# A mixer block's first stage: sums of z products written between the multiply and the low rows, tables last, latents in pairs of rows, and group sums by TensorE

## The chip, the core and the metric

The kernel runs on one core of a Trainium2 chip. A core has five engines that run side by side, each taking its own instructions in order: TensorE (PE in the profile; PEld is its weight load), VectorE (DVE), ScalarE (ACT), GpSimd (POOL) and SyncE (SP). SP and POOL issue DMAs, which 16 DMA engines carry out. An engine that needs another's result waits on a semaphore. The metric is the device time of one execution in microseconds, and the number given is the median over several executions.

## The reference

The block takes 512 latent tokens of width 2048 and 256 context tokens. A conditioning vector gives shift, scale and gate for every channel, and each token is normalized and modulated:

```
shift, scale, gate = split(silu(c) @ w_ada + b_ada, 3)
h = rmsnorm(x, norm_g) * (1 + scale) + shift
p = h @ w_in                       # 2048 -> 9216 columns
y_a = (attention(q, k, v of p and of the context) * silu(z_a)) @ w_proj_a
y_b = (fourier_mix(u_b) * silu(z_b)) @ w_proj_b
out = rmsnorm(x + gate * ((sig(g_a) * y_a + sig(g_b) * y_b) @ w_out), final_g)
```

Two groups of columns of `p` matter here: `u_b` (512 columns), which the Fourier mixing takes, and `z_b` (512 columns), its SiLU gate. The first stage computes both and, on the way, the modulated tokens `h` that all later stages read.

## The kernel before

The latents come in transposed, `xT`, so that channels lie on the 128 partitions. The 2048 channels are 16 blocks of 128, called rows here: row `kb` is a tile of 128 channels by 512 tokens. All products are made at close to float32 accuracy from three float32r matmuls: each operand is split into a high part (ScalarE, L176) and a low remainder (DVE, L177), and `mm3` (L327 to L329) adds high x high, high x low and low x high into one PSUM accumulator.

**Start.** `load_x` asks SP for the latents in the pieces that the list `XCH` gives: six loads of 2, 2, 4, 4, 2 and 2 rows. `token_norms` squares each row (ScalarE L522 and L526, for the second row of four of the pairs DVE L524), adds the two squares of a pair (DVE L527) and sums over partitions with a matmul by ones (L528). The roots are spread over the partitions (L539) and copied to `rx` (L709).

**Rows.** For each row `kb`, `modulate` runs 16 float32 matmuls of the conditioning vector with that row's part of `w_ada` (L551). The vector is padded to 32 columns and the matmuls fall on four groups of 32 partitions, so that the result, 256 columns wide, has four groups of partial sums, of which two partitions each (latents and context) hold numbers. ScalarE copies it out (`ado`, L567). `columns` has TensorE transpose its two halves (`turned`, L571), DVE adds the four groups (L579) and forms `gain` (L580) and `shift` (L582) for the row's 128 channels. The high part of the modulated row then comes from ScalarE, the low part from DVE: for rows 0 to 5 by `by_root` (L594), `row_hi` (L598) and `row_lo` (a multiply, L602, and the low part, L603), for rows 6 to 15 by `make_h` (a multiply, L609, ScalarE's L610, the low part, L611). For rows from 8 on `form_row` adds row differences that a later stage uses (L619 to L621).

**Products of the first stage.** `start_work` is a generator that multiplies the rows, as they become ready, with eight tiles of 128 columns: four of u, four of z. The u tiles have four PSUM accumulators of their own that stay open over all 16 rows (`pb`). The z tiles take turns on two accumulators (`pc`, `bank3`), for one row or two rows (for rows 12 to 15 four) at a time; each partial product is added to its running sum in SBUF (`part`) by `keep`: for row 0 ScalarE's copy (L631), later DVE's add (L633). That add frees the accumulator. `some(n)` runs the generator for `n` steps, of which a step is one tile. `hold` and `release` put one z sum off to a later place in the written order.

**The order.** In this stage the order of TensorE, ScalarE and DVE is the order in which the program is written (L701 and on). From row 6 on, the rows come in rounds of two, and a round has twelve steps: three, then the split of the next weight tile (`split_next`), the first row's modulation, two steps, its columns and its making, three steps, a split, the second row's modulation, one step (the first of four z tiles), its columns, its making and its differences, and three steps, the other z tiles. In the last round the splits of the Fourier tables (`split_table`, and the one of `dftc`) stand ahead of these three. SP issues the loads of `w_ada` and of the weight tiles in written order too, each when its buffer is free.

Of the kernel before, what the change touches and what calls it, by code (L numbers as in the profile page):

```python
# [10 lines left out]
F32 = mybir.dt.float32  # L11
F32R = mybir.dt.float32r
ACT = mybir.ActivationFunctionType
ALU = mybir.AluOpType
AX = mybir.AxisListType
# [3 lines left out]
P = 128  # L19
# [3 lines left out]
KK = D // P  # L23
# [78 lines left out]

XCH = [(0, 2), (2, 2), (4, 4), (8, 4), (12, 2), (14, 2)]


def start_pieces():
# [11 lines left out]
def block_kernel(ctx, tc, xT, ctx_rows, ctx_toks, x, c_row, w_ss, w_gate, vecs, qkg, rope, dft_c, dft_s,  # L120
                 w_start, w_g, w_pab, w_o, final_g, out):
    nc = tc.nc
# [29 lines left out]
    def uid(s):  # L152
        cnt[0] += 1
        return f"{s}{cnt[0]}"
# [278 lines left out]
    q = NGATE  # L433
# [61 lines left out]

    c2 = pap.tile([P, KK, 32], F32, name="c2")
    nc.vector.memset(c2, 0.0)
    rt = pap.tile([P, 1], F32, name="rt")
    ce = pap.tile([P, 2 * KK], F32, name="ce")
    with tc.issue_after(nc.scalar.activation(ce, cvt, ACT.Exp, scale=-1.0).ins):  # L500
# [10 lines left out]
    def token_norms():  # L511

        t = hm_tile([P, 2, T], F32, name=uid("nm"))
        pick, r = t[:, 0, :].rearrange("p (t c) -> p t c", t=4), t[:, 1, :P]
        nc.gpsimd.memset(pick, 0.0)
        for t in range(4):
            nc.gpsimd.memset(pick[32 * t : 32 * t + 1, t, :], 1.0)
        acc = bank2()
        for q in range(0, KK, 2):
            two = hm_tile([P, 2, T], F32, name=uid("sq"))  # L520
            a, b = two[:, 0, :], two[:, 1, :]
            nc.scalar.activation(a, xt[:, q, :], ACT.Square)  # L522
            if q in (4, 8, 10, 14):
                nc.vector.tensor_tensor(b, xt[:, q + 1, :], xt[:, q + 1, :], op=ALU.mult)  # L524
            else:
                nc.scalar.activation(b, xt[:, q + 1, :], ACT.Square)  # L526
            nc.vector.tensor_tensor(a, a, b, op=ALU.add)  # L527
            nc.tensor.matmul(acc, ones, a, start=q == 0, stop=q == KK - 2)  # L528

        for t in range(4):  # L530
            k = slice(32 * t, 32 * t + 32)
            nc.scalar.activation(r[k], acc[k, t * P : t * P + P], ACT.Sqrt, bias=eps_t[k, 0:1], scale=1.0 / D)
        nc.vector.reciprocal(r, r)
        return pick, r
# [22 lines left out]
    def modulate(kb, meanwhile=lambda: None):  # L557
        two[kb] = bank2()
        for h in range(2):
            matvec(kb, h)  # L560
        meanwhile()
        return taken(kb)
# [5 lines left out]

    def turned(sp, o):
        for i in range(2):  # L570
            nc.tensor.transpose(sp[:, P * i : P * i + P], o[:, P * i : P * i + P], ident)  # L571

    def columns(kb):
        sp, o = two.pop(kb)[:, 256:], o_of.pop(kb)
        turned(sp, o)
        if kb == 0:
            warm(3, o)
        r = pap.tile([P, 2, 2], F32, tag="ada_r", bufs=2, name=uid("adr"))
        nc.vector.tensor_reduce(r, sp.rearrange("p (h g r) -> p h r g", h=2, g=4)[:, :, 0:2, :], axis=AX.X, op=ALU.add)  # L579
        nc.vector.tensor_scalar(gain[:, kb, :], r[:, 1, :], bsc1[:, kb : kb + 1], ng[:, kb : kb + 1],  # L580
                                op0=ALU.add, op1=ALU.mult)
        last = nc.vector.tensor_scalar(shift[:, kb, :], r[:, 0, :], bada[:, kb : kb + 1], None, op0=ALU.add)  # L582
        return last

    rx0, y_of = [], {}
# [10 lines left out]
    def row_hi(kb):  # L596
        rows_of(kb)
        nc.scalar.activation(hhi[kb], y_of[kb], ACT.Identity, bias=shift[:, kb, 0:1], scale=gain[:, kb, 0:1])  # L598

    def row_lo(kb):  # L600
        v = xt[:, kb, :]
        nc.vector.tensor_scalar(v, y_of.pop(kb), gain[:, kb, 0:1], None, op0=ALU.mult)  # L602
        nc.vector.scalar_tensor_tensor(hlo[kb], v, shift[:, kb, 0:1], hhi[kb].bitcast(F32),  # L603
                                       op0=ALU.add, op1=ALU.subtract)

    def make_h(kb):
        rows_of(kb)
        v = xt[:, kb, :]
        nc.vector.scalar_tensor_tensor(v, v, gain[:, kb, 0:1], rx if kb else rx0[0], op0=ALU.mult, op1=ALU.mult)  # L609
        act = nc.scalar.activation(hhi[kb], v, ACT.Identity, bias=shift[:, kb, 0:1])  # L610
        return nc.vector.scalar_tensor_tensor(hlo[kb], v, shift[:, kb, 0:1], hhi[kb].bitcast(F32),  # L611
                                              op0=ALU.add, op1=ALU.subtract), act

    def form_row(j):

        a, b = xt[:, j, :], xt[:, j + 8, :]
        h, i = divmod(j, 4)
        d = pap.tile([P, 1], F32, tag="d", bufs=2, name=uid("d"))
        nc.vector.tensor_tensor(d, shift[:, j, 0:1], shift[:, j + 8, 0:1], op=ALU.subtract)  # L619
        nc.vector.tensor_tensor(whole["S3", h][:, i, :], a[:, :256], a[:, 256:], op=ALU.subtract)  # L620
        nc.vector.scalar_tensor_tensor(whole["Z5", h][:, i, :], a[:, 256:], d, b[:, 256:], op0=ALU.add, op1=ALU.subtract)  # L621
# [53 lines left out]
    def some(n):  # L675
        for _ in range(n):
            next(work)
# [10 lines left out]
    def split_next():  # L688
        e = next(e for e in ahead if e.out is None and e.kind != "raw")
        split_piece(e)  # L690
        e.raws = []
# [4 lines left out]
    def release():  # L696
        k = held.pop()
        keep(*k)

    E = mybir.EngineType  # L700
    with tc.manual_schedule(engines={E.PE}):  # L701
        norms = token_norms()
        two[0] = bank2()
        matvec(0, 0)
        rx0.append(spread(*norms))
        matvec(0, 1)
        with tc.manual_schedule(engines={E.Activation, E.DVE}):
            split_next()
            nc.scalar.copy(rx, rx0[0])  # L709
            by_root(0)  # L710
            taken(0)
            wada[2] = wada_load(2)
            load_start()
            columns(0)
            row_hi(0)
            row_lo(0)
            split_next()
            by_root(1)
            some(4)
            modulate(1, split_next)  # L720
            wada[3] = wada_load(3)
            load_start()
            some(2)
            columns(1)
            row_hi(1)
            row_lo(1)
            some(2)
            for kb in range(1, 4):
                k = kb + 1
                some(2)  # L730
                by_root(k)
                if kb > 1:
                    split_next()
                modulate(k)
                if kb < 3:
                    wada[k + 2] = wada_load(k + 2)
                    load_start()
                if kb == 1:
                    split_next()
                hold()  # L740
                some(2)
                columns(k)
                row_hi(k)
                release()
                row_lo(k)
                if kb == 3:
                    some(2)
                    by_root(5)
                    modulate(5)
                    for k in (6, 7):  # L750
                        wada[k] = wada_load(k)
                        load_start()
                    hold()
                    some(2)
                    columns(5)
                    row_hi(5)
                    release()
                    row_lo(5)
                else:
                    some(4)  # L760
            for kb in range(4, KK - 4, 2):
                some(3)
                split_next()
                for i in range(2):
                    k = kb + 2 + i
                    if i:
                        some(3)
                        split_next()
                    modulate(k)
                    if k + 2 < KK:  # L770
                        wada[k + 2] = wada_load(k + 2)
                        for _ in range(2 if k + 2 == KK - 3 else 1):
                            load_start()
                    some(2 - i)
                    columns(k)
                    make_h(k)
                    if k >= 8:
                        form_row(k - 8)
                if kb == KK - 6:
                    split_table(0)  # L780
                    split_from(get(("dftc", 0)), fch[:, 0, :], fch[:, 1, :])
                    load_start()
                some(3)
        for i in range(2):
            k = KK - 2 + i
            some(2)
            modulate(k)
            some(2 - i)
            columns(k)
            ins = make_h(k)  # L790
            with behind(ins):
                split_next()
                form_row(k - 8)
            if not i:
                load_start()
        some(1)
        some(8)
# [1162 lines left out]
```

## Time and profile before

| | us |
|---|---|
| median of 3 runs | 1317.34 (1315.83 to 1318.03) |
| profiled execution | 1314.17 |
| its span, first to last instruction | 1312.4 |
| TensorE busy | 1279.8 |
| DVE busy | 997.4 |
| ScalarE busy | 684.9 |

A row of the profile's timeline gives the start, the duration, the engine, the line, the operation, the tile written and the tiles read, the form, and how many instructions were merged into it; in brackets stands how long the engine had been idle and what ended that. A row of the waits gives the total, the number of times and the longest. A matmul's listed duration runs past the start of the next one, as matmuls are pipelined: back to back, those of 512 columns start 0.23 us apart. Tiles are named without numbers: `pd` holds a row's modulation, `pb` and `pc` are the accumulators above, `wa` is `w_ada`, `wr` a raw weight tile, `whi` and `wlo` its parts, and `s` a row's parts.

### The profile page before, as it was taken

How to read it: one execution, taken by the hardware profiler on the slowest of the kernel's cores; microseconds unless marked ns; L12 is line 12 of the kernel's file. 1: busy time of each engine (PE TensorE's matmuls, PEld its weight loads, DVE VectorE, ACT ScalarE, POOL GpSimd, SP SyncE). 2: the span in 40 equal slices, each digit the busy share in tenths (PEclk: the TensorE clock that was granted, in tenths of full speed). 3: DMA queues.
4: the chain of work that ended last, by engine and by line, in shares of the span. 5: the costliest groups of instructions: out<-in, count | busy, mean ns of one | idle time of the engine just before them, and what ended most of it. 6: DMA issues, size and time to landing. Idle time of an engine off the chain costs nothing.

```text
span 1312.4 us, 17551 instructions
## 1 busy us (share of the span) xinstructions
PE 1279.8 (98%) x6522; PEld 1047.6 (80%) x6522; DVE 997.4 (76%) x1303; ACT 684.9 (52%) x1079; POOL 167.8 (13%) x220
## 2 busy tenths in 40 slices
PE   6998999999999999999999999999999999999997
PEld 3665798888888888888888888888888888888885
DVE  5656699979788697667777756687888867887676
ACT  5222555555555555444345454666667645565544
POOL 0000011020112101011011020011110212221210
PEclk9999999999999999999999999999999999999999
DMA  9988566899798888976869897567872899998985
GB/s 385 372 334 328 190 183 174 256 209 295 203 264 266 253 314 254 324 207 166 260 207 265 294 232 252 196 200 234 264 231 91 222 246 239 253 216 229 218 207 173
DMA packets 103622, 318.54 MB, mean 243 GB/s; under 512 B 9808, under 2 KB 32976, under 8 KB 99184
## 3 DMA queue, kind: packets, MB, share of 16 engines
q1 hardware_dynamic: 54480, 197.86, 41.4%
q0 software_dynamic: 26736, 97.14, 34.3%
q10 hardware_dynamic: 22320, 22.42, 5.0%
q8 instruction: 51, 0.84, 0.2%
q14 instruction: 35, 0.29, 0.1%
HBM read 283.30 MB, written 34.09 MB: 242 GB/s over the span
## 4 chain that ended last, share of the span: by engine, by line
PE 91%; DVE 4%; ACT 2%; issue 1%; DMA 1%; SPq 0%; ACTq 0%; DVEq 0%
PE banks L327 10%; PE banks L328 10%; PE banks L329 10%; PE x L329 9%; PE x L328 9%; PE x L327 9%; PE y L329 7%; PE y L327 7%; PE y L328 7%; PE banks L1448 2%; PE pd L551 2%; PE pb L327 2%; PE pb L329 1%; PE pb L328 1%; PE pc L327 1%
## 5 line engine op out<-in xcount | busy, mean ns | idle before, releaser
L176 ACT ACTIVATE whi<-R 128x1024 fp32r<-128x1024 f32 x138 | 145.7, 1058 | 142.2 <-PE banks L329 53.5
L177 DVE TENSOR_TENSOR wlo<-R,whi 128x1024 fp32r<-128x1024 f32 x138 | 167.8, 1221 | 57.0 <-ACT whi L176 56.7
L177 DVE TENSOR_TENSOR wlo<-wr,whi 128x1024 fp32r<-128x1024 f32 (+1 forms) x122 | 147.3, 1212 | 63.6 <-ACT whi L176 63.0
L176 ACT ACTIVATE whi<-wr 128x1024 fp32r<-128x1024 f32 (+1 forms) x122 | 127.5, 1050 | 114.3 <-PE y L329 37.9
L327 PE MATMUL banks<-whi,s 128*128 128x512 f32 x396 | 157.0, 397 | 2.4 <-DVE ev L1015 1.5
L329 PE MATMUL banks<-whi,s 128*128 128x512 f32 x396 | 155.1, 392 | 0.0
L328 PE MATMUL banks<-wlo,s 128*128 128x512 f32 x396 | 155.1, 392 | 0.0
L327 PE MATMUL x<-whi,s 128*128 128x512 f32 x356 | 138.8, 390 | 0.0
L328 PE MATMUL x<-wlo,s 128*128 128x512 f32 x356 | 138.5, 389 | 0.0
L329 PE MATMUL x<-whi,s 128*128 128x512 f32 x356 | 138.5, 389 | 0.0
L329 PE MATMUL y<-whi,s 128*128 128x512 f32 x308 | 119.8, 389 | 0.5 <-DVE s L177 0.5
L327 PE MATMUL y<-whi,s 128*128 128x512 f32 x308 | 120.0, 389 | 0.2 <-DVE cxe L1168 0.2
L328 PE MATMUL y<-wlo,s 128*128 128x512 f32 x308 | 119.8, 389 | 0.0
L280 POOL DMA_DIRECT2D R<-in_w_g x64 | 56.0, 874 | 418.7 <-DVE wlo L177 261.1
L176 ACT ACTIVATE s<-wr 128x512 fp32r<-128x512 f32 (+2 forms) x95 | 61.1, 675 | 66.2 <-DMA wr<-cf_d 16.1
L177 DVE TENSOR_TENSOR s<-wr,s 128x512 fp32r<-128x512 f32 (+2 forms) x95 | 67.9, 747 | 28.8 <-ACT s L176 28.0
L327 PEld LDWEIGHTS banks<-whi,s 128*128 128x128 f32 x396 | 74.4, 188 | 17.9 <-ACT whi L176 1.9
L329 PEld LDWEIGHTS banks<-whi,s 128*128 128x128 f32 x396 | 74.4, 188 | 15.4
L328 PEld LDWEIGHTS banks<-wlo,s 128*128 128x128 f32 x396 | 74.5, 188 | 14.0 <-DVE wlo L177 0.2
L328 PEld LDWEIGHTS x<-wlo,s 128*128 128x128 f32 x356 | 66.8, 188 | 13.9 <-DVE wlo L177 0.2
L329 PEld LDWEIGHTS x<-whi,s 128*128 128x128 f32 x356 | 66.8, 188 | 13.9
L327 PEld LDWEIGHTS x<-whi,s 128*128 128x128 f32 x356 | 66.8, 188 | 13.8
(310 smaller groups left out, 2823.1 us busy)
## 6 DMA issues: line engine op xcount, KB each, us to landing
wr<-in_w_g SPq DMA_DIRECT2D x128, 512.0 KB, 5.3
wa<-in_w_ss SPq DMA_DIRECT2D x32, 1024.0 KB, 8.0
R<-in_w_g POOLq DMA_DIRECT2D x64, 512.0 KB, 7.0
R<-in_w_g SPq DMA_DIRECT2D x32, 512.0 KB, 5.7
wr<-in_w_gate SPq DMA_DIRECT2D x32, 512.0 KB, 4.9
wr<-in_w_o SPq DMA_DIRECT2D x24, 512.0 KB, 7.7
R<-in_w_o POOLq DMA_DIRECT2D x24, 512.0 KB, 9.2
wr<-in_w_pab SPq DMA_DIRECT2D x20, 512.0 KB, 5.8
```

The lines of the kernel that those rows point to most:

```text
L176: first = nc.scalar.activation(hi, src, ACT.Copy)
L177: return first, nc.vector.tensor_tensor(lo, src, hi.bitcast(F32), op=ALU.subtract)
L280: nc.gpsimd.dma_start(chain[e.pc], e.nxt, accum_op=ALU.add)
L327: nc.tensor.matmul(o, ah, bh, start=start, stop=False, skip_group_check=cont)
L328: nc.tensor.matmul(o, ah, bl, start=False, stop=False, skip_group_check=cont)
L329: nc.tensor.matmul(o, al, bh, start=False, stop=stop, skip_group_check=cont)
L551: nc.tensor.matmul(acc[32 * j : 32 * j + 32], c2[:, n, :], w[:, k, :], start=n < 4, stop=n >= KK - 4)
L1448: nc.tensor.transpose(tp[:, k * P : (k + 1) * P], p[:, k * P : (k + 1) * P], ident)
```

## The change

Five edits, all in the first stage:

- `XCH`: the latents come in nine loads, seven of two rows and two of one row. DVE squares the second row of two pairs instead of four, ScalarE the others.
- `turned` and `columns`: a new tile `four` (128 by 2, made once from the identity) has a one wherever a partition's place in its group of 32 is the column's number. Two float32 matmuls with `four` as the moving operand replace the two transposes; they add the four groups on the way, DVE's L579 is gone, and `gain` and `shift` read PSUM.
- `row_lo` is cut in two: the multiply is now `scaled`, and in the rounds of rows 2 and 3 two of the four steps that followed the row stand between it and the low part.
- `make_h` takes a function that it calls between ScalarE's part and the low part. For the second row of each round from row 6 on, one of the three last steps stands there, one behind the low part, one behind the row differences, and the tables come after that.
- In the loop over rows 2 to 4 the weight split is always made inside `modulate`, ahead of ScalarE's copy; for row 2 it stood behind it and behind the issue of the next loads.

```diff
-XCH = [(0, 2), (2, 2), (4, 4), (8, 4), (12, 2), (14, 2)]
+XCH = [(2 * i, 2) for i in range(KK // 2 - 1)] + [(KK - 2, 1), (KK - 1, 1)]
...
+    four = pap.tile([P, 2], F32, name="four")
+    nc.vector.tensor_reduce(four, ident.rearrange("p (g r) -> p r g", g=4)[:, 0:2, :], axis=AX.X, op=ALU.add)
...
-            if q in (4, 8, 10, 14):
+            if q in (6, 10):
...
     def turned(sp, o):
         for i in range(2):
-            nc.tensor.transpose(sp[:, P * i : P * i + P], o[:, P * i : P * i + P], ident)
+            nc.tensor.matmul(sp[:, 2 * i : 2 * i + 2], o[:, P * i : P * i + P], four, start=True, stop=True)
...
-        r = pap.tile([P, 2, 2], F32, tag="ada_r", bufs=2, name=uid("adr"))
-        nc.vector.tensor_reduce(r, sp.rearrange("p (h g r) -> p h r g", h=2, g=4)[:, :, 0:2, :], axis=AX.X, op=ALU.add)
-        nc.vector.tensor_scalar(gain[:, kb, :], r[:, 1, :], bsc1[:, kb : kb + 1], ng[:, kb : kb + 1],
+        nc.vector.tensor_scalar(gain[:, kb, :], sp[:, 2:4], bsc1[:, kb : kb + 1], ng[:, kb : kb + 1],
                                 op0=ALU.add, op1=ALU.mult)
-        last = nc.vector.tensor_scalar(shift[:, kb, :], r[:, 0, :], bada[:, kb : kb + 1], None, op0=ALU.add)
+        last = nc.vector.tensor_scalar(shift[:, kb, :], sp[:, 0:2], bada[:, kb : kb + 1], None, op0=ALU.add)
...
-    def make_h(kb):
+    def make_h(kb, meanwhile=lambda: None):
         rows_of(kb)
         v = xt[:, kb, :]
         nc.vector.scalar_tensor_tensor(v, v, gain[:, kb, 0:1], rx if kb else rx0[0], op0=ALU.mult, op1=ALU.mult)
         act = nc.scalar.activation(hhi[kb], v, ACT.Identity, bias=shift[:, kb, 0:1])
+        meanwhile()
...
                 by_root(k)
-                if kb > 1:
-                    split_next()
-                modulate(k)
+                modulate(k, split_next)
                 if kb < 3:
                     wada[k + 2] = wada_load(k + 2)
                     load_start()
-                if kb == 1:
-                    split_next()
                 hold()
                 some(2)
                 columns(k)
                 row_hi(k)
                 release()
+                scaled(k)
+                if kb < 3:
+                    some(2)
                 row_lo(k)
...
                 else:
-                    some(4)
+                    some(2)
...
                     some(2 - i)
                     columns(k)
-                    make_h(k)
+                    make_h(k, lambda: some(i))
+                    some(i)
                     if k >= 8:
                         form_row(k - 8)
+                some(1)
                 if kb == KK - 6:
                     split_table(0)
                     split_from(get(("dftc", 0)), fch[:, 0, :], fch[:, 1, :])
                     load_start()
-                some(3)
```

More of the change, by code (lines that the diff above doesn't have):

```diff
@@ L598, in row_hi, with scaled @@
         nc.scalar.activation(hhi[kb], y_of[kb], ACT.Identity, bias=shift[:, kb, 0:1], scale=gain[:, kb, 0:1])
+    def scaled(kb):
+        nc.vector.tensor_scalar(xt[:, kb, :], y_of.pop(kb), gain[:, kb, 0:1], None, op0=ALU.mult)
     def row_lo(kb):
         v = xt[:, kb, :]
-        nc.vector.tensor_scalar(v, y_of.pop(kb), gain[:, kb, 0:1], None, op0=ALU.mult)
         nc.vector.scalar_tensor_tensor(hlo[kb], v, shift[:, kb, 0:1], hhi[kb].bitcast(F32),
                                        op0=ALU.add, op1=ALU.subtract)
-    def make_h(kb):
+    def make_h(kb, meanwhile=lambda: None):
         rows_of(kb)
@@ L715, in block_kernel @@
             row_hi(0)
+            scaled(0)
             row_lo(0)
@@ L725, in block_kernel @@
             row_hi(1)
+            scaled(1)
             row_lo(1)
@@ L757, in block_kernel @@
                     release()
+                    scaled(5)
                     row_lo(5)
                 else:
-                    some(4)
+                    some(2)
             for kb in range(4, KK - 4, 2):
```

## The prediction

> **What bounds the kernel now.** I read the page's first part, then busy time by stretch, then TensorE's waits, then the timeline at the longest of them.
>
> ```profile
> span 1312.4 us, 17551 instructions
> PE 1279.8 (98%) x6522; PEld 1047.6 (80%) x6522; DVE 997.4 (76%) x1303; ACT 684.9 (52%) x1079; POOL 167.8 (13%) x220
> ```
>
> TensorE (PE) is the bound: what shortens its busy or idle time shortens the span. The written order that changes covers the first 150 us.
>
> ```profile
> 24.30:73.86 49.56, 48.88 (x376) 32.62 (x376) 31.73 (x60) 16.77 (x26) 0.00 (x0) 1.00 0.97 389
> 73.86:150.22 76.36, 67.95 (x472) 46.99 (x471) 43.80 (x91) 20.26 (x31) 0.00 (x0) 0.96 0.67 259
> ```
>
> Columns: stretch, length, busy us of PE, weight loads, DVE, ACT, POOL, granted clock, DMA share, GB/s. The first stretch keeps PE full and DMA nearly full (0.97). The second leaves PE idle 8.4 of 76.4 us, at a clock below 1, with DMA at 0.67: there is room, and neither DVE (43.8) nor ACT (20.3) is full.
>
> ```profile
> PE pc L327 <- DVE part L633: 8.4, 4, 3.4
> PE y L329 <- DVE s L177: 0.5, 1, 0.5
> ```
>
> The first row (total, times, longest) is all of that idle time: four times PE waits for a z sum (L633), which empties one of the two pc accumulators. The second is PE's only wait between 165 and 300 us. So what the first stage saves reaches the later work.
>
> One of the four, at row 9:
>
> ```profile
> 89.46 0.75 DVE L609 SCALAR_TENSOR_TENSOR xt<-xt,gain,rx 128x512 f32<-128x512 f32 x1
> 89.50 0.39 PE L329 MATMUL pc<-s,wlo 128*128 128x512 f32 x1
> ...
> 90.89 0.39 PE L329 MATMUL pc<-s,wlo 128*128 128x512 f32 x1
> 91.00 0.75 DVE L611 SCALAR_TENSOR_TENSOR s<-xt,shift,s 128x512 fp32r<-128x512 f32 x1 [0.79 <-ACT s L610]
> ...
> 92.47 1.28 DVE L633 TENSOR_TENSOR part<-pc,part 128x512 f32<-128x512 f32 x2
> 93.21 0.50 PE L327 MATMUL pc<-s,whi 128*128 128x512 f32 x1 [1.93 <-DVE part L633]
> ```
>
> The second z product ends at 89.50 + 0.39 = 89.89, the third is issued to 90.89, and the fourth needs the second's accumulator. Its sum stands on DVE behind multiply (L609), a 0.79 us wait for ScalarE, low row (L611) and the row differences (L619 to L621). PE starts again 0.74 us after the pair of sums begins.
>
> **The change, part by part.** *Sums between multiply and low rows (L609, L611).* The multiply ends at 89.46 + 0.75 = 90.21, after the second product. Its sum takes half of 1.28, some 0.65 us, and fits the 0.79 us in which DVE waits for ScalarE: it ends at about 90.9, the low row stays near 91.0, and the fourth product can follow the third at 90.89 + 0.23 = 91.12. The third sum comes after the low row, the fourth after the differences; their accumulators are next wanted a whole round later. All four waits go. In start-to-start time each is worth slightly more than its row: 90.89 to 93.21 is 2.32, less a step of 0.23 is 2.09, that is 0.16 more than 1.93, as a matmul's listed end lies past the next one's start. Together 8.4 + 4 x 0.16 = 9.0 us. What is late next? Nothing: behind the moved sums stand only the differences and the next split, and PE takes those a round later.
>
> *Tables last.* The longest wait is the one where the table splits stand ahead of the sums:
>
> ```profile
> 128.15 1.22 DVE L177 TENSOR_TENSOR fsq<-wr,fsq 128x1024 fp32r<-128x1024 f32 x1
> ...
> 129.62 1.28 DVE L633 TENSOR_TENSOR part<-pc,part 128x512 f32<-128x512 f32 x2
> 130.36 0.79 PE L327 MATMUL pc<-s,whi 128*128 128x512 f32 x1 [3.41 <-DVE part L633]
> ```
>
> This wait is already in the 9.0. It does more:
>
> ```profile
> 132.00:134.00 2.00, 2.00 (x7) 1.51 (x6) 0.68 (x1) 0.00 (x0) 0.00 (x0) 0.50 0.84 322
> ...
> 111.03 0.50 PE L327 MATMUL pc<-s,whi 128*128 128x512 f32 x1 [1.93 <-DVE part L633]
> 116.54 0.50 PE L327 MATMUL pb<-s,whi 128*128 128x512 f32 x1
> ...
> 137.99 0.50 PE L327 MATMUL pb<-s,whi 128*128 128x512 f32 x1
> ```
>
> After the 3.41 us wait PE runs at half clock. The same work from wait to next product takes 116.54 - 111.03 = 5.51 us one round earlier and 137.99 - 130.36 = 7.63 here: 2.1 us, gone with the wait. No wait of 1.93 us lowered the clock. [...]
>
> Two loads wait on SP for the tables' buffers:
>
> ```profile
> 129.39 0.80 SPq L212 DMA_DIRECT2D wr<-in_w_start  x2
> ...
> 146.59 1.99 ACT L176 ACTIVATE whi<-wr 128x1024 fp32r<-128x1024 f32 x2
> ...
> wr<-in_w_start SPq DMA_DIRECT2D x2, 512.0 KB, 5.9
> ```
>
> Behind them nothing is issued until PE is further on. Their tiles are split 17 us later; with PE 5.7 us ahead (3.6 + 2.1) and the tables some 2 us later against the sums, 9 us remain for a landing of 5.9. I cost it at nothing, covered by that slack of 3 us; below that the splits, and PE behind them, would wait.
>
> *Rows 2 to 4.* Same move, smaller waits, of which I count the largest:
>
> ```profile
> 41.12 0.39 PE L651 MATMUL pb<-s,wlo 128*128 128x512 f32 x1
> ...
> 41.94 0.50 PE L650 MATMUL pc<-s,whi 128*128 128x512 f32 x1 [0.42 <-DVE part L633]
> ```
>
> 0.82 less a step of 0.23: 0.6 us. The low row becomes later by one sum, 0.65 us, but is read only by the last two products of the next pair. One weight split now stands ahead of ScalarE's copy of row 2's sums:
>
> ```profile
> 36.31 0.37 ACT L567 COPY ado<-pd 128x256 f32<-128x256 f32 x1 [2.76 <-PE pd L551]
> 36.58 1.06 ACT L176 ACTIVATE whi<-wr 128x1024 fp32r<-128x1024 f32 x1
> ```
>
> It fills 1.06 of 2.76 us idle if its load has landed, and delays the copy, the turned sums and PE by up to 1.3 us if not: 0 to +1.3, once. I take 0: at 36.58 it did not wait for its load.
>
> *Group sums by TensorE (L571, L579).* Each row's two transposes become two matmuls with two moving columns. A float32 matmul here is two passes: L539's four calls appear eight times below.
>
> ```profile
> 65.10 0.39 PE L329 MATMUL pb<-s,wlo 128*128 128x512 f32 x1
> ...
> 65.33 0.38 PE L571 MATMUL pd<-ident,ado 128*128 128x128 f32 x2
> ...
> 65.78 0.40 PE L328 MATMUL pb<-s,whi 128*128 128x512 f32 x1
> ...
> 19.57 0.97 PEld L539 LDWEIGHTS pc<-s 128*128 128x128 f32 x8 [2.10 <-issue]
> ...
> L571 PE MATMUL pd<-ident,ado 128*128 128x128 f32 x32 | 6.1, 273 | 0.5 <-ACT ado L567 0.5
> L539 PEld LDWEIGHTS pc<-s 128*128 128x128 f32 x5 | 0.6, 192 | 0.0
> ```
>
> From 65.10 to 65.78 there are two steps of 0.23 and the transposes: they cost 0.22 us. The weight load sets a pass: (0.97 - 0.19) / 7 = 0.11 us start to start. Four passes cost 0.44, so +0.22 a row, 15 rows on PE's path (row 0's lie in an idle stretch): +3.3 us. Bounds: 0, if short passes hide; four unhidden passes, among the rivals. I take the load's row: it has the same operand.
>
> ```profile
> 65.82 0.17 DVE L579 TENSOR_REDUCE adr<-pd 128x4 f32<-128x16 f32 x1 [2.04 <-PE pd L571]
> 66.03 0.29 DVE L580 TENSOR_SCALAR gain<-adr,bsc,small 128x2 f32<-128x2 f32 x1
> ```
>
> DVE loses the reduction, 0.21 us a row from its start to gain's, which pays for two more passes in the chain to the row: no gain there. Gain and shift now read the accumulator. [...]
>
> *Latents in pairs.*
>
> ```profile
> 1.18 2.89 SPq L465 DMA_DIRECT2D xt<-in_xT  x6
> ...
> 13.78 0.63 ACT L522 ACTIVATE s<-xt 128x512 f32<-128x512 f32 x1
> 15.09 0.69 DVE L527 TENSOR_TENSOR s<-s 128x512 f32<-128x512 f32 x1
> ```
>
> Nine loads instead of six, 0.48 us of SP each: later issues slip 1.4 us. DMA is full behind them, so their landing should not. Pairs let the squares begin earlier, so that no backlog stands before the last pair; its second row is there by 13.78 as before, ScalarE squares the first just ahead of it, and two squares of 0.5 to 0.6 us end near 14.8, where the add can start instead of at 15.09. I take -0.3; bounds -0.6 (one square) and +1.4 (the slip).
>
> Faster rows could run into loads where DMA is full:
>
> ```profile
> 57.36 1.19 SPq L465 DMA_DIRECT2D wa<-in_w_ss  x2
> wa<-in_w_ss SPq DMA_DIRECT2D x1, 1024.0 KB, 9.6
> 67.73 1.93 PE L551 MATMUL pd<-wa,c 128*32 128x256 f32 x32
> ```
>
> The second load is issued near 58.2 and lands at 67.8; its half of the sums starts near 68.7. Up to there the change moves PE by -0.3 - 0.6 + 6 x 0.22 = +0.4, so the margin of 0.9 us stays.
>
> **Sum.** -9.0 - 2.1 - 0.6 - 0.3 + 3.3 = -8.7 us. The profiled execution took 1314.17 us (span 1312.4, 1.8 around it), 3.2 below the median of the runs: 1305.5 for it, 1308.6 for the median 1317.34.
>
> **Rivals.**
> *No clock dip in the timed runs.* [...] Without it -6.6: 1310.7. For it: the dip appears once, after one wait. Against: the wait is nearly twice any other.
> *Given back later.* PE's wait of 0.5 us on the splits shows a later stretch where DVE is as slow as PE. Arriving earlier could wait there. From half given back, 1313.0, to all. Against: those splits start from loads that move along.
> *The sum does not fit the gap.* If it starts after the low row, only the differences (91.75 to 92.47, 0.7 us) and the tables (128.15 to 129.62, 1.5 us) leave its path: 3 x 0.7 + 1.5 + 2.1 + 0.9 - 3.3 = 3.3 us: 1314.0. Against: multiply ends after the second product.
> *Slower: unhidden passes.* If a two-column pass is too short to cover the next load, it costs load plus matmul, 0.19 + 0.27 = 0.46: four cost 1.86, +1.64 a row, +24.6 in 15. Net +12.6: 1329.9. Slower from (12.0 / 15 + 0.22) / 4 = 0.26 us a pass. Against: transposes run at 0.11.
>
> **How the numbers follow.** Forecast 0.62, no dip 0.15, given back 0.09 (0.04 of it within 0.2%, 2.6 us, which is what a measurement of this kernel can tell from no change), sum does not fit 0.06, unhidden passes 0.08. Faster 0.88, same 0.04, slower 0.08. Range: low 1305.0, passes hidden (-3.3) and start at its bound (-0.3); high 1312.8, past no dip, with the copy's 1.3 or the start's slip, up to half given back: 0.8.
>
> **What would show it.** Right: no wait of pc on L633 above 0.3 us; granted clock 1 from 130 to 137; L633 between L609 and L611 in odd rows from 7; four L571 passes 0.11 apart, 0.44 us a row; second stage about 9 us earlier with waits as before. Wrong: passes 0.26 or more apart; PE waiting for wa or ScalarE's copy near 36 or 68 us; a half-clock stretch elsewhere; DVE waiting on a product with PE behind it.

## The result, and the profile after

The changed kernel takes 1307.96 us (median of 6 runs, 1305.18 to 1310.19) where the kernel before took 1317.13 beside it (6 runs, 1313.71 to 1320.1): a ratio of 0.993 (95% interval 0.9911 to 0.9949). The forecast was 1308.6. Measured a second time, it was 1308.45 against 1316.24, a ratio of 0.9939 (0.992 to 0.9958).

The profiled execution took 1307.42 us, 0.5 below its median; that of before lay 3.0 below the median of these runs, so that the two traces differ by 6.75 us and the medians by 9.2. The busy times on the page of the kernel after:

```profile
PE 1280.5 (98%) x6554; PEld 1051.1 (81%) x6554; DVE 993.6 (76%) x1286; ACT 687.5 (53%) x1081; POOL 170.1 (13%) x220
```

PE is as busy as before; its idle time has shrunk. The span went from 1312.4 to 1305.7, by 6.7 us. Busy time by stretch (columns as before: stretch, length, PE, weight loads, DVE, ACT, POOL, clock, DMA share, GB/s), over the same work: 73.80 and 139.49 are the starts of the matmuls that started at 73.86 and 150.22 before.

```profile
24.32:73.80 49.48, 49.48 (x390) 34.81 (x391) 31.61 (x55) 17.38 (x26) 0.00 (x0) 1.00 0.99 400
73.80:139.49 65.69, 65.69 (x489) 47.81 (x487) 42.21 (x83) 20.10 (x30) 0.00 (x0) 1.00 0.77 297
```

The second stretch was 76.36 us long with PE busy for 67.95 of them; now it is 65.69 us long, PE has no gap in it, and the clock is 1. PE's waits from 0 to 170 us, after (total, times, longest):

```profile
PE pd L530 <- DVE s L529: 7.1, 1, 7.1
PE pc L541 <- DVE s L535: 1.6, 1, 1.6
PE pd L573 <- ACT ado L569: 0.5, 1, 0.5
```

All three lie before the first product. No wait on a z sum (now L636) is left, and none on `wa` or on a weight tile. Row 9 on DVE's timeline, after:

```profile
87.97 0.75 DVE L611 SCALAR_TENSOR_TENSOR xt<-xt,gain,rx 128x512 f32<-128x512 f32 x1
88.88 0.69 DVE L636 TENSOR_TENSOR part<-pc,part 128x512 f32<-128x512 f32 x1 [0.16 <-PE pc L329]
89.52 0.75 DVE L614 SCALAR_TENSOR_TENSOR s<-xt,shift,s 128x512 fp32r<-128x512 f32 x1
```

and on PE's:

```profile
89.82 0.39 PE L329 MATMUL pc<-s,wlo 128*128 128x512 f32 x1
90.05 0.39 PE L327 MATMUL pc<-s,whi 128*128 128x512 f32 x1
```

The sum (L636) stands between the multiply (L611) and the low row (L614) and ends at 89.57; PE steps on at 90.05, 0.23 us after its last product, where it used to lose 2.09.

To place the difference I compare the starts of the same matmuls. The stage's end is here the matmul that starts at 172.64 us before and 161.60 after. That is 11.04 us earlier, more than the 8.7 of the forecast. The rest is lost again: from there to the matmul that starts at 440 us before, the kernel before needs 267.33 us and the kernel after 269.49; from there to the last matmul 862.99 and 864.78. Of the second, 1.3 us lie between the matmuls at 600 and 800 us of before; the other traces of the kernel after, below, lose 0.1 to 0.5 there, and I did not follow it up. The first of the two losses has one place, in PE's waits from 400 to 450 us of the kernel after, a wait that the kernel before does not have:

```profile
PE x L328 <- DVE wlo L177: 1.9, 1, 1.9
```

### The profile page after: what moved, and what is told of

Same layout as the page of the kernel before. It is cut to its first block, busy times and chain, and to the rows that moved or that the text cites. A ratio compares the mean times of both kernels' runs of the same rounds, so it can differ in the third digit from the quotient of the medians.

```text
span 1305.7 us, 17605 instructions
## 1 busy us (share of the span) xinstructions
PE 1280.5 (98%) x6554; PEld 1051.1 (81%) x6554; DVE 993.6 (76%) x1286; ACT 687.5 (53%) x1081; POOL 170.1 (13%) x220
## 4 chain that ended last, share of the span: by engine, by line
PE 88%; DMA 4%; DVE 3%; ACT 2%; issue 2%; POOL 0%; SPq 0%; DVEq 0%; ACTq 0%; POOLq 0%
PE banks L327 9%; PE banks L328 9%; PE banks L329 9%; PE x L328 8%; PE x L329 8%; PE x L327 8%; PE y L329 7%; PE y L327 7%; PE y L328 7%; PE banks L1454 2%; PE pd L553 2%; DMA s<-yb_d 2%; PE pb L327 2%; PE pb L329 1%; PE pb L328 1%
## 5 line engine op out<-in xcount | busy, mean ns | idle before, releaser
L329 PEld LDWEIGHTS x<-whi,s 128*128 128x128 f32 x356 | 66.8, 188 | 13.9
```

Of the source, the lines that this page charges most:

```text
L329: nc.tensor.matmul(o, al, bh, start=False, stop=stop, skip_group_check=cont)
```

## The experiments

Each ratio is to the kernel before as measured beside that kernel: 1317.13 us for the first row of the kernel after, and a median of 1316.24 for all others. The kernel of the last row ran once and has no ratio. The three right-hand columns come from one trace each. "Stage" is the start of the matmul named above, "first" that of the first product (24.30 before), "middle" the stretch from the stage's end to the matmul at 440 us of before.

| kernel | median, us (runs) | ratio (interval) | first | stage | middle |
|---|---|---|---|---|---|
| before | 1317.13 (6) | 1 | 24.30 | 172.64 | 267.33 |
| after | 1307.96 (6) | 0.993 (0.9911 to 0.9949) | 24.32 | 161.60 | 269.49 |
| transposes back | 1301.99 (6) | 0.9882 (0.9859 to 0.9906) | 24.48 | 158.76 | 269.48 |
| order alone | 1301.98 (4) | 0.9891 (0.9857 to 0.9926) | 24.45 | 158.73 | 267.74 |
| group sums alone | 1316.56 (10) | 1.0005 (0.9986 to 1.0025) | 24.63 | 170.67 | 268.54 |
| tables alone | 1314.3 (10) | 0.9976 (0.9959 to 0.9993) | 24.37 | 170.02 | 268.81 |
| transposes, tables ahead of the last z tile | 1301.89 (4) | 0.9901 (0.9875 to 0.9927) | 24.39 | 158.77 | 267.92 |
| after, again | 1308.45 (6) | 0.9939 (0.992 to 0.9958) | 24.25 | 161.54 | 271.49 |
| rows 2 to 4 as before | 1306.81 (1) | – | 24.15 | 162.40 | 269.24 |

**The transposes back.** The changed kernel, with the group sums undone:

```diff
-            nc.tensor.matmul(sp[:, 2 * i : 2 * i + 2], o[:, P * i : P * i + P], four, start=True, stop=True)
+            nc.tensor.transpose(sp[:, P * i : P * i + P], o[:, P * i : P * i + P], ident)
...
+        r = pap.tile([P, 2, 2], F32, tag="ada_r", bufs=2, name=uid("adr"))
+        nc.vector.tensor_reduce(r, sp.rearrange("p (h g r) -> p h r g", h=2, g=4)[:, :, 0:2, :], axis=AX.X, op=ALU.add)
```

> The changed kernel with the two transposes and DVE's reduction put back; order, tables and pairs stay. My theory (order and clock gain about 14 us by the end of the first stage, the four passes cost 0.22 us in each of 14 rows where TensorE does not wait): the stage ends 3.1 us earlier than in the changed kernel, about 14.1 us before the kernel before, median about 1304.9. Rival (the reduction has to leave DVE for the moved sums to fit the gap between multiply and low row): waits on the z sums come back, 0.2 us or more in each of four rounds, and the median stays at 1308 or above.

The stage ended 2.84 us sooner, at 158.76. Aligned by matmuls, the gain is 0.22 to 0.23 us at each of the rows 2 to 15. One of these rows on PE's timeline, first of the kernel after:

```profile
45.30 0.39 PE L329 MATMUL pc<-s,wlo 128*128 128x512 f32 x1
45.53 0.50 PE L573 MATMUL pd<-four,ado 128*128 128x2 f32 x4
...
46.21 0.39 PE L328 MATMUL pb<-s,whi 128*128 128x512 f32 x1
```

and with the transposes back:

```profile
45.32 0.39 PE L329 MATMUL pc<-s,wlo 128*128 128x512 f32 x1
45.55 0.38 PE L571 MATMUL pd<-ident,ado 128*128 128x128 f32 x2
...
46.00 0.40 PE L328 MATMUL pb<-s,whi 128*128 128x512 f32 x1
```

From the last product ahead of it to the second behind it (45.30 to 46.21 and 45.32 to 46.00) the four passes take 0.91 us and the two transposes 0.68: four steps of 0.11 against two, although the passes have two moving columns. The reduction that DVE gets back brings no wait on a z sum back. PE's waits from 0 to 170 us, transposes back:

```profile
PE pd L528 <- DVE s L527: 7.1, 1, 7.1
PE pc L539 <- DVE s L533: 1.6, 1, 1.6
PE pb L653 <- ACT s L598: 0.6, 2, 0.3
PE pd L571 <- ACT ado L567: 0.5, 1, 0.5
```

New against the kernel after are two waits of 0.3 us for ScalarE's high rows (L598), which the passes had covered. So within the stage the group sums are a loss of about 3 us, as expected, and this kernel beats both that were given. Its median, expected at 1304.9, is 1302: 6.0 us below that of the kernel after, twice what the stage explains. The last experiments go after the rest.

**Order alone.** The kernel before with the new written order and nothing else; against the kernel of the last experiment it has the old list of loads:

```diff
-XCH = [(2 * i, 2) for i in range(KK // 2 - 1)] + [(KK - 2, 1), (KK - 1, 1)]
+XCH = [(0, 2), (2, 2), (4, 4), (8, 4), (12, 2), (14, 2)]
...
-            if q in (6, 10):
+            if q in (4, 8, 10, 14):
```

> The kernel before with the new written order alone: sums between multiply and low rows, tables last, the split inside the modulation; six loads of latents and transposes as before. My theory (pairs are worth nothing: the trace of the changed kernel starts its first row 0.02 us later than before): equal to the run with transposes within 0.2 us at the first row and at the end of the stage. Rival (pairs gain what I predicted, 0.3 us, or cost through later issues): the first row starts 0.3 us later or up to 1.4 us earlier than in the run with transposes.

First product and stage's end are within 0.03 us of the kernel with pairs: in these two traces the latents in pairs are worth nothing. From one execution to the next the first product varies by more than that. It starts at 24.06 to 24.48 us in the eight traces of kernels with pairs and at 24.30 to 24.84 in the six without, so that a gain or loss of some tenths of a microsecond isn't excluded. The order by itself brings the stage 13.9 us forward. The start shows why the pairs do so little. ScalarE's squares of rows 4 and 6 in the kernel before:

```profile
8.73 1.15 ACT L522 ACTIVATE s<-xt 128x512 f32<-128x512 f32 x2 [1.34 <-DMA xt<-in_xT]
```

and from row 4 on in the kernel after:

```profile
1.17 4.54 SPq L465 DMA_DIRECT2D xt<-in_xT  x9
...
7.80 0.63 ACT L524 ACTIVATE s<-xt 128x512 f32<-128x512 f32 x1
...
12.92 0.63 ACT L524 ACTIVATE s<-xt 128x512 f32<-128x512 f32 x1 [0.65 <-DMA xt<-in_xT]
...
13.98 0.62 ACT L524 ACTIVATE s<-xt 128x512 f32<-128x512 f32 x1
...
15.15 0.69 DVE L529 TENSOR_TENSOR s<-s 128x512 f32<-128x512 f32 x1 [0.35 <-ACT s L528]
```

The squares of row 4 do begin earlier, at 7.80 instead of 8.73. But SP takes 4.54 us for nine issues instead of 2.89 for six, and the last row, whose load is issued at 5.24 and lands 9.0 us later, arrives at 14.24; before, the last load was issued at 3.62 and landed 10.1 us later, at 13.75. So the squares of the last pair begin at 13.98 instead of 13.78, and the last add starts at 15.15, where it was 15.09.

**Group sums alone.** The kernel before with `four` in place of the transposes:

```diff
-            nc.tensor.transpose(sp[:, P * i : P * i + P], o[:, P * i : P * i + P], ident)
+            nc.tensor.matmul(sp[:, 2 * i : 2 * i + 2], o[:, P * i : P * i + P], four, start=True, stop=True)
```

> The kernel before with the group sums by TensorE alone. My theory (TensorE's passes count only where it does not wait for DVE; where it does, DVE's lost reduction shortens the wait): +0.22 us in rows 4, 5, 6, 8, 10, 12, 14 and 15, about -0.2 in rows 2, 7, 9, 11 and 13, together +0.8 us, median 1318. Rival (0.22 us in each of 15 rows, as my prediction counted): +3.3 us, median 1320.4.

No change that can be measured (1.0005), against 0.8 us expected and 3.3 in the rival. In the trace the passes cost 0.22 us a row also here, but each of the four waits on the z sums became 0.42 to 0.44 shorter in start-to-start time, since DVE reaches its sums without the reduction and PE arrives later: a net 0.1 us up to the product that started at 130.36. The longest wait was still there with 2.98 us, and yet the clock stayed up in this execution. By stretch:

```profile
125.90:129.32 3.42, 1.91 (x9) 1.24 (x7) 2.63 (x6) 1.98 (x3) 0.00 (x0) 1.00 1.00 408
129.32:132.73 3.41, 1.95 (x8) 1.61 (x9) 2.25 (x5) 0.00 (x0) 0.00 (x0) 1.00 0.85 285
132.73:136.14 3.41, 3.41 (x39) 1.99 (x38) 0.44 (x1) 0.35 (x1) 0.00 (x0) 1.00 0.38 154
```

The idle time falls 1.51 us into the first stretch and 1.46 into the second; no row has half clock. That is the earlier stage end of 170.67. It need not be so each time: seven of the ten timed executions show a mean granted clock of 0.996 or less, and every trace without a half-clock stretch ahead of its last product shows 0.997 or 0.998.

**Tables alone.** The kernel before with the three z tiles of the last round ahead of the tables:

```diff
+                some(3)
                 if kb == KK - 6:
...
-                some(3)
```

> The kernel before with the table splits alone moved behind the three z tiles of the last round; sums stay behind the row differences. My theory (the long wait alone lowers the clock): the wait of 3.4 us falls to 1.9 as in the rounds before it, the half-clock stretch goes, together 1.5 + 2.8 = 4.3 us less, median 1312.8. Rival (the clock falls from any such wait by where its window lies): the wait falls by 1.5 us and a half-clock stretch stays or moves to another of the four waits, 1.5 us less, median 1315.6.

My theory fell: with the wait cut from 3.41 to 1.93 us the clock still dropped.

```profile
126.62 0.39 PE L329 MATMUL pc<-s,wlo 128*128 128x512 f32 x1
128.94 0.50 PE L327 MATMUL pc<-s,whi 128*128 128x512 f32 x1 [1.93 <-DVE part L633]
129.28 0.40 PE L328 MATMUL pc<-s,whi 128*128 128x512 f32 x1
...
129.76 0.41 PE L327 MATMUL pc<-s,whi 128*128 128x512 f32 x1
129.99 0.60 PE L328 MATMUL pc<-s,whi 128*128 128x512 f32 x1
```

The listed durations grow at 129.99, the fifth product behind the wait. By stretch of the same kernel:

```profile
126.60:130.01 3.41, 1.48 (x7) 0.88 (x6) 2.75 (x6) 1.35 (x3) 0.00 (x0) 1.00 1.00 415
130.01:133.42 3.41, 3.41 (x9) 2.26 (x7) 2.16 (x3) 0.00 (x0) 0.00 (x0) 0.50 0.14 56
```

Here all of the wait falls into one stretch of 3.41 us, which is idle for 1.93 of it (57%), and the next stretch runs at half clock. Against the 2.98 us of the group sums alone, which left the clock up, what differs is where the wait falls in these stretches; its length does not tell the two apart.

**The tables ahead of the last z tile.** The kernel with the transposes back, and in it:

```diff
-                some(1)
                 if kb == KK - 6:
...
+                some(1)
```

> The changed kernel with the transposes put back, and the table splits ahead of the last z tile's sum instead of behind it. Theory (with the sums moved, the last z sum's accumulator is not wanted for several microseconds, so the place of the tables is worth nothing): the stage ends within 0.2 us of that of the kernel with transposes, no wait of pc, clock 1. Rival (tables last is a part of the gain of its own): a wait of 1.5 us on the z sum at the end of the last round, with or without a half-clock stretch of 2 to 3 us.

The stage's end is 158.77 against 158.76. DVE's timeline in this kernel:

```profile
121.58 1.22 DVE L177 TENSOR_TENSOR fsq<-wr,fsq 128x1024 fp32r<-128x1024 f32 x1
...
123.05 0.68 DVE L636 TENSOR_TENSOR part<-pc,part 128x512 f32<-128x512 f32 x1
```

The last sum stands behind the tables, until 123.05, and PE does not wait for it. With the other sums moved into the rows, tables ahead of the last one cost nothing; the 3.6 and 2.1 us that I had put down to the longest wait and its clock are there without the edit that the prediction called tables last.

**Rows 2 to 4 as before.** The changed kernel with the old order there:

```diff
-                modulate(k, split_next)
+                if kb > 1:
+                    split_next()
+                modulate(k)
...
+                if kb == 1:
+                    split_next()
...
-                if kb < 3:
-                    some(2)
                 row_lo(k)
...
-                    some(2)
+                    some(4)
```

> The changed kernel with rows 2 and 3 written as before: all four steps behind the low row, and row 2's split behind ScalarE's copy. Theory (the waits of 0.6 and twice 0.2 us come back, shortened by the reduction that DVE no longer has and with TensorE's own 0.22 us a row absorbed in them): stage 0.6 us longer by row 4, the same from there on. Rival (with the reduction gone the old order of these rows is as good): 0.2 us or less.

The stage ended 0.80 us later than after, or 0.97 counted from the first product, where 0.6 was expected: steps of 0.46 and 0.11 at row 2, 0.28 and 0.11 at row 3. ScalarE's copy of row 2 does not show: the wait it could have made does not appear in the changed kernel.

**The kernel after, and the kernel before, again.** Both unaltered, to see what varies.

> The changed kernel, unaltered, on the chip of the other runs of this call. Theory (the wait of 1.9 us on a weight load near 426 us is a load that lands late in some executions, whatever the first stage does): the end of the first stage 11.0 us before that of the kernel before, with steps at the same places as in the first trace; the wait near 426 us there or not. Rival (the earlier first stage causes it): the wait is there again with 1.5 us or more. Against the kernel with transposes the first theory expects 3 us more in the medians too.

> The kernel before, unaltered, for a second trace of its clock. Theory (the clock is halved at the end of a 3.41 us window in which TensorE sat idle more than about 0.55 of the time, the windows run on from wherever they started, and it comes back after a window without idle time): the same four waits of 1.1, 1.9, 1.9 and 3.4 us; every window of idle share 0.57 or more is followed by a half-clock stretch of 3.4 or 6.8 us, none of 0.53 or less is. Rival (the 3.4 us wait alone lowers the clock, each time): one stretch of 6.8 us after the last wait whatever the windows show.

The stage of the kernel after repeated to 0.06 us (161.54); the middle did not: 271.49 instead of 269.49. The kernel before had its half clock at the same place, but for 3.41 us instead of 6.83, and a second one where its first trace had none:

```profile
126.93:130.34 3.41, 0.55 (x3) 0.13 (x1) 3.13 (x7) 1.50 (x3) 0.00 (x0) 1.00 1.00 416
130.34:133.75 3.41, 2.86 (x7) 2.29 (x8) 1.09 (x2) 0.00 (x0) 0.00 (x0) 0.50 0.98 356
133.75:137.16 3.41, 3.41 (x40) 1.95 (x39) 0.69 (x1) 0.00 (x0) 0.00 (x0) 1.00 0.17 67
...
922.20:925.64 3.44, 0.80 (x4) 0.33 (x2) 0.05 (x1) 1.40 (x3) 1.08 (x2) 1.00 0.38 149
925.64:929.00 3.36, 2.28 (x7) 1.99 (x8) 3.09 (x6) 2.08 (x5) 0.54 (x1) 0.50 0.85 268
929.00:932.40 3.40, 3.40 (x13) 2.92 (x12) 1.32 (x2) 0.99 (x2) 0.98 (x2) 0.50 1.02 339
```

That execution took 1321.1 us. The first half of the expectation held here: both stretches idle for 57% or more are followed by half clock, and none of 53% or less is. The other half, that the clock comes back after a stretch without idle time, did not: the first half-clock stretch here is idle for 0.55 of 3.41 us, and the clock is back behind it.

**Is the loss in the middle chance?** Two more traces of the kernel after and one more each of the two kernels 6 us below it, all unaltered.

> The changed kernel, unaltered, for one more trace behind the first stage. From the end of the stage (the matmul that starts at 161.6 in its first trace) to the matmul that starts at 440 in the kernel before, its two traces took 269.49 and 271.49 us, those with the transposes back 267.74, 267.92 and 269.48, the kernel before 267.33 and 267.48. Theory: the group sums on TensorE bring the kernel to the load near 426 us in a phase in which it lands late each time, so this is 269 to 272 us again and the whole time 1307 to 1309. Rival: how late that load lands is chance from run to run, whatever the first stage does: then values below 268.5 appear here as well, with a time of 1305 to 1306.

> As the run two before this one, once more. Theory: 269 to 272 us from the end of the stage to the matmul at 440, 1307 to 1309 in all. Rival: below 268.5 in one of the two, 1305 to 1306 in all.

> The changed kernel with the two transposes and VectorE's reduction back, unaltered, for one more trace. Its first took 158.76 us to the end of the stage and 269.48 from there to the matmul at 440, the one trace with transposes that is as long as those of the changed kernel. Theory, by which the group sums set it: that was chance and this is 267.5 to 268.5, 1301 to 1302 in all. Rival, by which the latents in pairs or nothing in the first stage sets it: 269 to 272 again, 1303 to 1305 in all.

> The kernel before with the written order alone, unaltered, for one more trace. Its first took 158.73 us to the end of the stage, 267.74 from there to the matmul at 440, and 1300.92 in all. Theory: 267.5 to 268.5 us in that stretch again, and 1300 to 1302 in all. Rival: by chance it can be 269 to 272 here, with 1303 to 1306 in all.

| | whole time | stage | middle |
|---|---|---|---|
| after, third | 1305.38 | 161.64 | 269.39 |
| after, fourth | 1309.82 | 161.63 | 272.94 |
| transposes back, second | 1300.97 | 158.51 | 267.30 |
| order alone, second | 1301.51 | 158.77 | 267.81 |

The four traces of the kernel after have 269.4 to 272.9 us in the middle, the five of kernels with the new order and transposes 267.3 to 267.9 four times and 269.48 once. So the loss is not chance alone. The expectations for the kernel after were too narrow, though: the middle came as the theory had it in the third trace and longer in the fourth, the whole time below its 1307 to 1309 us in the one and above it in the other. The place of the loss is a load that DVE needs for a later weight tile. DVE's timeline of the kernel after:

```profile
422.56 1.23 DVE L265 TENSOR_TENSOR wr<-R,wr 128x1024 f32<-128x1024 f32 x1 [3.54 <-DMA wr<-in_w_g]
...
425.23 2.50 DVE L265 TENSOR_TENSOR wr<-R,wr 128x1024 f32<-128x1024 f32 x2 [0.84 <-DMA wr<-in_w_g]
427.64 1.22 DVE L177 TENSOR_TENSOR wlo<-wr,whi 128x1024 fp32r<-128x1024 f32 x1
```

and of the kernel with the transposes back, second trace:

```profile
418.26 1.23 DVE L265 TENSOR_TENSOR wr<-R,wr 128x1024 f32<-128x1024 f32 x1 [3.52 <-DMA wr<-in_w_g]
...
420.00 2.35 DVE L265 TENSOR_TENSOR wr<-R,wr 128x1024 f32<-128x1024 f32 x2
```

Between these two, PE is 3.1 us apart at the stage's end, but the first of the rows is 4.3 us later (422.56 - 418.26) and the second 5.2 (425.23 - 420.00): against PE the first is 1.2 us later and the second about 2, and PE waits 1.9 us for the split at 427.64. In the second and the fourth trace of the kernel after this wait lowered the clock as well; the fourth:

```profile
428.85:432.26 3.41, 0.93 (x4) 0.80 (x5) 3.34 (x3) 0.38 (x1) 0.00 (x0) 1.00 0.30 119
432.26:435.67 3.41, 3.41 (x10) 2.62 (x9) 3.41 (x5) 0.01 (x1) 1.56 (x2) 0.50 0.67 163
```

Two things go with their lateness. One is the group sums. The load that the second row waits for and the one issued right behind it, from issue to landing in the kernel after:

```profile
wr<-in_w_g SPq DMA_DIRECT2D x2, 512.0 KB, 7.9
```

and with the transposes back, second trace:

```profile
wr<-in_w_g SPq DMA_DIRECT2D x2, 512.0 KB, 6.6
```

These two loads take 7.2 to 8.3 us in all six traces of kernels with the group sums, the group sums alone and rows 2 to 4 as before among them, and 6.4 to 6.7 in all eight with transposes. The other is the time at which they are issued, which varies with either: counted from the stage's end, the first of the two is issued at 254.4 to 255.2 us in six of the eight traces with transposes, and at 256.0 and 256.8 in the tables alone and in the first trace with the transposes back, the two with a middle of 268.81 and 269.48. PE's longest wait there is 0.9 to 2.5 us in the six traces with group sums, 1.2 and 1.8 in those two and at most 0.3 in the other six. Why the loads take longer in kernels with the group sums, and what sets the time of their issue, stays open. I did not try to issue them earlier.

The timed runs point the same way. Five of the twelve executions of the kernel after show a mean clock of 0.996 or less, lower than in any trace without a half-clock stretch ahead of its last product; of the fourteen executions of the three kernels with the new order and transposes none does. So half clock behind the stage is probably a part of the 6 us between their medians; how large a part was not measured.

## Why the prediction was right, and where it was not

The time came out 0.6 us from the forecast, and the mechanism that carries most of the sum, the moved z sums, held. That the number is so close is luck: two errors offset each other. The stage gained 2.3 us more than I summed, and in the trace 4.0 were lost again later.

| term | forecast | measured |
|---|---|---|
| four waits on the z sums | -9.0 | -9.05, and -0.44 for slower first steps behind them |
| half clock | -2.1 | -2.85 |
| rows 2 to 4 | -0.6 | -1.3 |
| pairs, start | -0.3 | 0 in this trace |
| group sums | +3.3 | +3.0 |
| entry into the Fourier products, near 164 us of before | 0 | -0.3 |
| not placed | | -0.1 |
| stage | -8.7 | -11.04 |
| later | 0 | +2.2 in the middle, +1.8 behind it |

*The waits.* Right, by the mechanism: the sum fits the gap that ScalarE leaves, its low row is no later, and all four go. The rival in which the sum does not fit fell with the row at 88.88. I missed 0.11 us a wait: the first product after a wait takes a step of 0.34, not 0.23 (128.94 to 129.28 above).

*The half clock.* The term was mis-sized. I compared the stretch behind the longest wait with the one a round earlier as the same work; it has 12 products, the earlier one 15, and the three missing steps of 0.23 are 0.7 us. The mechanism I gave, a wait of 3.41 us trips the clock and 1.93 does not, was wrong as a rule: with the tables alone 1.93 us tripped it, and with the group sums alone 2.98 us did not. In all fourteen traces the clock changes at multiples of 3.41 us from where its record begins, and what a wait does to it goes with the share of such a stretch that it leaves idle: 57% was enough (below). The rival of no dip in the timed runs fell as far as the record can tell: both traces of the kernel before have the dip at 130 us, and 30 of its 35 timed executions beside the experiments have a mean clock of 0.996 or less, below every trace without a dip. The dip's length and further dips vary from one execution to the next.

*Rows 2 to 4.* I counted the largest wait alone. The sum of the small steps around it is twice as much. Undone alone, the order of rows 2 and 3 was worth 0.8.

*Tables last.* I booked nothing for it apart from the waits, and the slack of their loads held: PE waits for neither table. By itself it gains 1.9 us in the medians; behind the moved sums it moves the stage's end by 0.01.

*Pairs.* The step that failed is the landing. I had the last row there by 13.78 as before, and it landed at 14.24; rows from 4 on were squared earlier, but the add behind the last pair was not. Neither end of my bounds (-0.6, +1.4) was reached.

*Group sums.* The price of a pass, 0.11 us, taken from the weight load of another line, was right to 0.01, and the rival of unhidden passes, with 0.26 or more, is out. Row 1's share did not show, for with the transposes PE waits for ScalarE there. Gain and shift from the accumulator are not dearer: gain has a median of 0.278 us from the accumulator, and 0.289 from SBUF before; shift takes 0.211 us in the mean, and 0.222 before.

*What is late next.* "Nothing" held in the stage and failed behind it. The given-back rival had the right kind of place, DVE splitting weights behind loads, but I ruled it out because "those splits start from loads that move along". They came 1.2 to 2 us later against PE. Of the 11.04 us some 4 were lost in that trace, 2.2 of them up to the matmul at 440 us of before and 1.8 behind it, where only the stretch of 1.3 is known and its cause is not. The wait of 0.5 us between 165 and 300 us that I quoted for it did stay as it was.

## What to carry to other kernels

An addition that frees an accumulator belongs into the gap in which its engine waits anyway, ahead of work that nobody needs yet; the written order, of which that move is the main part, made the whole gain here. A small matmul costs its passes: four float32 passes with two moving columns took 0.44 us, and the reduction they save was worth nothing once the sums had moved, so take such a part back and measure the rest. The best kernel of the study is the written order with the transposes kept, at 1302 us, 1.1 to 1.2% below the kernel before. When a stage gains, look for the first late load behind it before adding the gain to the total.

## What the runs showed of the hardware

- *The clock changed in steps of 3.41 us, and a stretch idle for 57% was enough to halve it.* In the first trace of the kernel before the record of the clock begins at 10.24 us, and the clock changes at 129.71, 136.53 and 1307.31: 35, 37 and 380 times 3.413 us later. Cut into such stretches, the fourteen traces have six between the first and the last product in which PE was idle for 57% or more, and each was followed by half clock; none with 53% or less was, the highest such one being the stretch around the third of the kernel before's long waits. Behind the last product the clock halves in all fourteen traces, each time after a stretch that is idle for 68% or more: at 1299.07 in the first trace of the kernel after, behind a stretch idle for 82%. What lies between 53 and 57% no trace shows. From the first trace of the kernel before:

```profile
109.23:112.64 3.41, 1.61 (x7) 1.34 (x8) 2.35 (x6) 0.51 (x1) 0.00 (x0) 1.00 0.98 396
126.29:129.71 3.42, 0.66 (x3) 0.19 (x2) 3.04 (x7) 1.60 (x3) 0.00 (x0) 1.00 1.00 414
129.71:133.12 3.41, 2.76 (x7) 2.19 (x8) 1.19 (x2) 0.00 (x0) 0.00 (x0) 0.50 0.95 322
133.12:136.53 3.41, 3.41 (x15) 2.01 (x17) 0.69 (x1) 0.00 (x0) 0.00 (x0) 0.50 0.20 79
```

  So a wait of 1.93 us (tables alone) halved the clock for 3.41 us and one of 2.98 us (group sums alone) left it alone, by where it fell. The half clock lasted one stretch four times and two stretches twice; what brings it back is not settled.
- *A small matmul did not get cheaper with fewer columns.* In the kernel after a float32 matmul with two moving columns took two passes of 0.11 us, each the same step as a transpose with 128 columns in the kernel with the transposes back.
- *The same load can take longer in a changed kernel.* Two loads of 512 KB, issued near 417 us in the kernel after, took 7.2 to 8.3 us to land in the six traces of kernels with the group sums and 6.4 to 6.7 in the eight without, though the last group sum is done some 280 us earlier. Why is open.
